# Memory norm and bias table in the second output part of the first feed-forward, memory tiles read once more and split in the third; a later norm row and other weight splits in the second feed-forward

## The chip, the cores and the metric

The kernel runs on one core of a Trainium2 chip. The metric is the device time of one execution in microseconds (us); smaller is better. A core has TensorE (PE) for matrix products, VectorE (DVE), ScalarE (ACT) and GpSimd (POOL) for elementwise work, and SyncE (SP), which here only issues DMAs. The engines run side by side and meet at semaphores.

## The reference

One decoder layer on x (512 tokens, 1024 features) in float32:

```python
x = x + 0.5 * swiglu(rms_norm(x, norm_ffn1_w), ffn1_w_in, ffn1_w_out)      # d_ff 2816
x = x + hybrid_mixer(rms_norm(x, norm_mix_w), ...)                         # SSD heads and attention heads
x = x + memory_cross_attention(rms_norm(x, norm_cross_w), rms_norm(mem, norm_mem_w), w_cq, w_ck, w_cv, w_co)
x = x + 0.5 * swiglu(rms_norm(x, norm_ffn2_w), ffn2_w_in, ffn2_w_out)
return rms_norm(x, norm_final_w)
```

Three details matter. `mem` has 256 rows of 1024 features, and its norm and its key product `rms_norm(mem) @ w_ck` depend on nothing that is computed before them. The attention heads add a bias looked up by relative position from a table of 32 buckets and 8 heads, and subtract a second softmax scaled by `lam`, a scalar made from four small parameter vectors. The root mean square that each norm divides by needs all 1024 features of a token.

## The kernel before, in words

**Layout and arithmetic.** Activations lie transposed, features on partitions: x is 8 tiles of 128x512. Every product is made in three float32r passes from a high and a low part of both operands (`mm3`, L261): high by high, high by low, low by high. So every weight tile (128x1024, 512 KB) is loaded raw by SP into `wr` (6 buffers), its high part `wh` is made by ACT (L149, 3 buffers) and its low part `wl` by DVE from `wr` and `wh` (L150, 3 buffers). An activation is split the same way, `gh` and `gl` for the gated values of a feed-forward, `hnh` and `hnl` for a normed x, `hm` for the memory.

**First feed-forward.** Its 22 tiles of hidden features go in thirds of 8, 8 and 6 (`THIRDS`). A third has quads (L223), products in a Strassen manner: seven products `m1`, `t`, `t+m3`, `m2`, `m7`, `m3`, `t` of summed weights with summed activations. The weight sums are made by accumulating DMAs on POOL's queue (L219) and by DVE (L245, L247), and before the second product ACT copies the first, `qb<-qa` (L241). Behind the last quad comes the gate chain: `gate` on DVE (L385), `th` on ACT (L386), two more steps on DVE (L387, L389), then `gh` on ACT and `gl` on DVE, two tiles of each. Then the output part of that third: for each of 8 output tiles o a product `po` of `nf` weight blocks with the `nf` gated tiles, 24 matmuls of 512 columns in the first two thirds and 18 in the last, and an update of x[o]. The gated tiles of the last quad are only needed by the last quarter or third of each product.

**Statistics.** `Stat` (L318) collects squares: ACT makes `nacc` or `nsq` (L328, L331), DVE adds (L332). `finish` turns the sum into a row: PE sums over partitions into `nps`, DVE makes `nv` (L302), POOL raises it to the power -0.5 (`ncol`, L304), and 2.5 us of planned PE time later `row_of` makes `ch` and `cl` on DVE, two diagonal tiles `ndiag` (one on DVE, one on POOL, L315), two matmuls `nrow`, and ACT copies `nrow` into `row` (L343). `normed` (L348) does this for the mixer's norm and then makes 8 pairs `hf`, `hnh`, `hnl`.

**Beside the third output part** the function `beside` (L457) spawns two chains of small work. `prepare` (L480) loads `lamv`, `rel_sb` and `hot`, makes `lam`, and makes the bias table: one matmul `prel` (L501), an ACT copy `rel_row` (L503), a small DMA to `rel_d` in DRAM and a DMA of 2.5 MB from there to `rel_z` (L506), both on POOL's queue; the attention reads `rel_z` later. `memory_prep(hm, True)` (L862) reads the 8 memory tiles (128x256) by DMAs on POOL's queue, each held in program order behind the accumulating DMAs issued so far (`last_sum`), adds their squares to `st_mem`, splits each into `hm`, and finishes the memory's norm row. Later, in the mixer, `memory_prep(hm2, False)` reads the tiles again.

**After it** comes `memory_keys` (L875): 8 products `pck` of 24 matmuls with 256 columns. It needs `hm` from the start and `st_mem.row` only at `ckf` (L882), after the products. While PE does these keys, the mixer's norm is made by `normed`, spawned at the last x update with a delay of 3.0. Then the mixer begins with the products `pq` of `hn`.

**Second feed-forward.** The norm's row is finished by `st_2.finish()`, spawned 3.0 after the last update (L1008), while the first quad runs; the row is needed at the first gate. Its last third is laid out by token so that the final norm is at hand: `Close.load` splits the left halves of the first two raw weights into `wfh` and `wfl`, `Close.finish` (L1036) splits the other left halves in its loop over f, and then all six right halves.

**What sets the order.** Dense generators yield after each group of matmuls; `Order` (L53) keeps a planned PE time `od.t`, which each matmul advances, and steps the spawned chains when their due time has come. A tile scheduler then orders the instructions of PE, DVE, ACT and POOL by its own estimate, and each engine executes its list strictly in that order. SP alone keeps the order in which the code issues. `tc.issue_after(i)` makes the scheduler place an instruction behind i in the list.

## Time and profile before

| | |
|---|---|
| median of 3 runs | 1359.58 us (1359.15 to 1363.79) |
| profiled execution | 1359.36 us, of which the profile's span is 1357.6 us |
| mean granted TensorE clock | 0.993 |
| PE busy in the span | 1325.9 us, 98% |
| DVE, ACT, POOL busy | 952.6, 631.9, 106.5 us |
| DMA traffic | 166.84 MB, mean 123 GB/s |

The table of busy times says which engine could bound the kernel; which one does, and where it is held up, is told by the table of PE's waits (what each wait ended on, and how long), by windows cut at the stages (busy time of each engine in a stretch of the span, with the clock granted to TensorE) and by the timeline (start and duration of each instruction, and in brackets the idle time before it and what ended it). In these views a line number is that of the kernel, and L140, L149 and L150 are helpers, so the tile names tell the instructions apart. The span leaves out 1.76 us of the execution, before the first and after the last recorded instruction.

### The profile page before, as it was taken

To read this page: it belongs to the slowest core of one execution; us is meant where nothing else is said; L and a number is where in the kernel's file an instruction comes from. 1 tells how busy PE (TensorE), PEld (TensorE's weight loads), DVE (VectorE), ACT (ScalarE), POOL (GpSimd) and SP (SyncE) were. 2 spreads that over 40 slices of the span, in tenths; PEclk is the share of its full clock that TensorE was granted. 3 is DMA by queue.
4 is the path that set the end of the run, shared out by engine and by line. 5 is a ranking of instruction groups with operands and counts; after the bars stand their busy time and mean duration, and the time that the engine had idled before them with its cause. 6 is when DMAs were issued, how large, how long until landed. Compare 5 with 4: busy or idle time off the path is not lost.

```text
span 1357.6 us, 19860 instructions
## 1 busy us (share of the span) xinstructions
PE 1325.9 (98%) x7829; PEld 1150.3 (85%) x7829; DVE 952.6 (70%) x1480; ACT 631.9 (47%) x1069; POOL 106.5 (8%) x130
## 2 busy tenths in 40 slices
PE   8999999998989999999999999999999999999997
PEld 7888999897777778877788887889889989998995
DVE  6874787577767577647867877656788757875765
ACT  6442454244444464536644656434445424542544
POOL 1000000011020001000011031000001000000000
PEclk9999999999989999999999999999999999999999
DMA  7435574463542213432163665321347645745631
GB/s 265 111 120 127 125 201 133 117 187 103 203 154 70 84 51 61 141 109 62 40 124 102 94 123 157 109 78 63 83 104 181 179 129 128 195 137 124 174 106 62
DMA packets 50157, 166.84 MB, mean 123 GB/s; under 512 B 6464, under 2 KB 6872, under 8 KB 50064
## 3 DMA queue, kind: packets, MB, share of 16 engines
q1 hardware_dynamic: 40704, 134.57, 31.2%
q0 software_dynamic: 9360, 31.01, 13.6%
q8 instruction: 61, 1.00, 0.3%
q14 instruction: 32, 0.26, 0.1%
HBM read 163.41 MB, written 4.77 MB: 124 GB/s over the span
## 4 chain that ended last, share of the span: by engine, by line
PE 88%; DVE 3%; DMA 2%; ACT 2%; issue 1%; POOL 1%; POOLq 0%; ACTq 0%; DVEq 0%
PE po L140 17%; PE qb L211 12%; PE pm L140 8%; PE qe L211 7%; PE qa L211 7%; PE pxbc L140 7%; PE pq L140 3%; PE pk L140 3%; PE pcq L140 3%; PE pv L140 3%; PE pz L140 3%; PE pf L140 2%; PE pck L140 2%; PE pg L140 2%; PE pu L140 2%; PE ps L140 2%
## 5 line engine op out<-in xcount | busy, mean ns | idle before, releaser
L149 ACT ACTIVATE wh<-wr 128x1024 fp32r<-128x1024 f32 (+2 forms) x285 | 292.2, 1028 | 391.0 <-PE po L140 129.5
L150 DVE TENSOR_TENSOR wl<-wr,wh 128x1024 fp32r<-128x1024 f32 (+2 forms) x285 | 339.2, 1191 | 105.0 <-ACT wh L149 102.8
L140 PE MATMUL po<-gh,wh 128*128 128x512 f32 x304 | 119.4, 395 | 4.3 <-ACT gh L149 2.4
L140 PE MATMUL po<-gl,wh 128*128 128x512 f32 x304 | 119.0, 394 | 0.0
L140 PE MATMUL po<-gh,wl 128*128 128x512 f32 x304 | 118.8, 393 | 0.0
L211 PE MATMUL qa<-hmh,wl 128*128 128x256 f32 x304 | 86.3, 284 | 0.0
L211 PE MATMUL qa<-hml,wh 128*128 128x256 f32 x304 | 86.0, 283 | 0.0
L211 PE MATMUL qa<-hmh,wh 128*128 128x256 f32 x304 | 86.0, 283 | 0.0
L441 DVE TENSOR_TENSOR upd<-po,row 128x512 f32<-128x512 f32 x40 | 27.7, 691 | 78.8 <-PE po L140 78.8
L140 PEld LDWEIGHTS po<-gh,wh 128*128 128x128 f32 x304 | 57.3, 190 | 18.0 <-ACT gh L149 4.6
L140 PEld LDWEIGHTS po<-gl,wh 128*128 128x128 f32 x304 | 57.6, 190 | 13.1 <-DVE gl L150 1.2
L140 PEld LDWEIGHTS po<-gh,wl 128*128 128x128 f32 x304 | 57.6, 189 | 12.0 <-DVE wl L150 0.3
L211 PEld LDWEIGHTS qa<-hmh,wl 128*128 128x128 f32 x304 | 58.3, 192 | 0.4 <-DVE wl L150 0.4
L211 PEld LDWEIGHTS qa<-hml,wh 128*128 128x128 f32 x304 | 58.3, 192 | 0.2
L211 PEld LDWEIGHTS qa<-hmh,wh 128*128 128x128 f32 x304 | 58.3, 192 | 0.2
L140 PE MATMUL pxbc<-hnh,wh 128*128 128x512 f32 x128 | 52.3, 409 | 0.0
L140 PE MATMUL pxbc<-hnh,wl 128*128 128x512 f32 x128 | 50.3, 393 | 0.0
L140 PE MATMUL pxbc<-hnl,wh 128*128 128x512 f32 x128 | 50.3, 393 | 0.0
L219 POOL DMA_DIRECT2D wr<-in_f2q x22 | 19.1, 870 | 363.3 <-DVE wl L150 110.4
L628 ACT ACTIVATE ec<-ec,mn 128x512 f32<-128x512 f32 (+3 forms) x64 | 35.4, 556 | 25.5 <-DVE mn L627 25.5
L211 PE MATMUL qb<-s12h,wh 128*128 128x256 f32 x152 | 43.3, 285 | 3.5 <-ACT qb L241 3.5
L211 PE MATMUL qe<-s12h,wh 128*128 128x256 f32 x152 | 43.3, 285 | 1.2 <-ACT s12h L149 1.1
(375 smaller groups left out, 3780.4 us busy)
## 6 DMA issues: line engine op xcount, KB each, us to landing
wr<-in_f2q SPq DMA_DIRECT2D x55, 512.0 KB, 4.2
wr<-in_f1q SPq DMA_DIRECT2D x40, 512.0 KB, 4.0
wr<-in_f2q POOLq DMA_DIRECT2D x22, 512.0 KB, 6.3
wr<-in_f2o SPq DMA_DIRECT2D x22, 512.0 KB, 4.2
wr<-in_f1q POOLq DMA_DIRECT2D x16, 512.0 KB, 6.4
wr<-in_f1o SPq DMA_DIRECT2D x16, 512.0 KB, 4.2
wr<-in_wxbc SPq DMA_DIRECT2D x16, 512.0 KB, 3.5
wr<-in_f1i SPq DMA_DIRECT2D x8, 512.0 KB, 6.9
```

The source lines that it names most:

```text
L140: nc.tensor.matmul(out, w, x, start=start, stop=stop)
L149: S.activation(hi, src, AF.Copy),
L150: V.tensor_tensor(lo, src, hi.bitcast(F32), ALU.subtract),
L211: nc.tensor.matmul(out, a_[:, wc], b_, start=first and f == 0 and kp == 0 and j == 0, stop=kp == n - 1 and j == 2, skip_group_check=True)
L219: last_sum[:] = [G.dma_start(raw, m, accum_op=ALU.add).ins]
L441: V.tensor_tensor(upd, po, row4, ALU.mult)
L628: S.activation(ec[:, :n], ec[:, :n], AF.Exp, bias=mn, scale=-1.0, accum_out=sm[c][:, i : i + 1])
```

## The change

Five edits, all in the order of the work; the number of matmuls, of ACT and of DVE instructions stays the same (7674, 951 and 1482 in the program), POOL issues 8 DMAs more.

1. `prepare` and the memory's norm are spawned at the second output part (`ti == 1`) and no more at the third. The memory's preparation is cut in two: `memory_norm` reads the 8 tiles, squares and sums them and makes the row; `memory_prep(hm)` reads the 8 tiles again and splits them, at the third output part as before. With `hm2` the tiles are now read three times in all.
2. The tiles' DMAs stand behind the last accumulating DMA as before (`last_sum`), and their work on ACT and DVE stands behind the last weight split (`recent`).
3. `rel_row` goes; ACT copies `prel` into the first 8 partitions of `hot`.
4. `Stat.finish` takes the distance between `nps` and `nrow` as an argument: 6.0 for the memory, 8.0 for the second feed-forward's norm, which is spawned 5.0 instead of 3.0 after the last update. For the mixer's norm it stays 2.5.
5. In `Close.finish` four of the six right halves are split within the loop over f, the other two after it.

```diff
     def load_w(src, n=D):
...
-            split_into(hi, lo, raw)
+            recent[:] = [i.ins for i in split_into(hi, lo, raw)]
         return hi, lo
+
+    @contextmanager
+    def behind(ins):
+        with ExitStack() as after:
+            for i in ins:
+                after.enter_context(tc.issue_after(i))
+            yield
...
-        def finish(self):
+        def finish(self, apart=2.5):
...
-            yield 2.5
+            yield apart
...
     def beside(ti):
-        if ti == len(THIRDS) - 1:
+        if ti == 1:
             od.spawn(prepare())
-            od.spawn(memory_prep(hm, True))
+            od.spawn(memory_norm())
+        elif ti == 2:
+            od.spawn(memory_prep(hm))
...
-        rel_row = s2("rel_row", shape=(8, T))
-        S.activation(rel_row, prel, AF.Copy, scale=-8.0)
-        nc.gpsimd.dma_start(rel_d[:, :T], rel_row)
+        S.activation(hot[:8], prel, AF.Copy, scale=-8.0)
+        nc.gpsimd.dma_start(rel_d[:, :T], hot[:8])
...
-    def memory_prep(dst, first):
+    def memory_tile(k):
+        mk = s2("mem", shape=(P, MEM))
+        with behind(last_sum):
+            nc.gpsimd.dma_start(mk, a["memT"][k])
+        return mk
+
+    def memory_norm():
         for k in range(KT):
-            mk = s2("mem", shape=(P, MEM))
-            with tc.issue_after(last_sum[0]):
-                nc.gpsimd.dma_start(mk, a["memT"][k])
-            if first:
+            mk = memory_tile(k)
+            with behind(recent):
                 st_mem.add(mk)
-            dst.append(split("hm", mk, par[:, C_MEM + k : C_MEM + k + 1], True))
             yield 2.0
-        if first:
-            yield 3.0
-            yield from st_mem.finish()
+        yield 3.0
+        yield from st_mem.finish(6.0)
+
+    def memory_prep(dst):
+        for k in range(KT):
+            mk = memory_tile(k)
+            with behind(recent):
+                dst.append(split("hm", mk, par[:, C_MEM + k : C_MEM + k + 1], True))
+            yield 2.0
...
-            od.spawn(st_2.finish(), 3.0)
+            od.spawn(st_2.finish(8.0), 5.0)
...
+            w2 = []
             for f in range(nf):
                 if f + 2 < nf:
                     w.append(split("wf", self.raw[f + 2][:, :T]))
+                if f > 1:
+                    w2.append(split("wf", self.raw[f - 2][:, T:]))
...
-            w = [split("wf", self.raw[f][:, T:]) for f in range(nf)]
+            w2 += [split("wf", self.raw[f][:, T:]) for f in range(nf - 2, nf)]
```

What this does to the engines' lists shows at three places. Two `wh` in a row belong to two consecutive weight tiles.

ACT, at the end of the last quad of the second third: the splits of the first three output weights, the gate's `th`, the splits of the last gated tiles. Before:

```order
L149 ACTIVATE wh_2203<-wr_2201 128x1024
L149 ACTIVATE wh_2237<-wr_2235 128x1024
L149 ACTIVATE wh_2271<-wr_2269 128x1024
L386 ACTIVATE th_2185<-gate_2184 128x1024
L149 ACTIVATE gh_2192<-th_2185 128x512
L149 ACTIVATE gh_2196<-th_2185 128x512
```

And after the change, where `nacc` and `nsq` are squares of two memory tiles and `hot<-prel` is the copy of the bias row:

```order
L149 ACTIVATE wh_2203<-wr_2201 128x1024
L335 ACTIVATE nacc_2233<-mem_2231 128x256
L338 ACTIVATE nsq_2249<-mem_2247 128x256
L393 ACTIVATE th_2185<-gate_2184 128x1024
L149 ACTIVATE gh_2192<-th_2185 128x512
L149 ACTIVATE gh_2196<-th_2185 128x512
L511 ACTIVATE hot_2226<-prel_2291 8x512
L149 ACTIVATE wh_2267<-wr_2265 128x1024
```

Two weight splits moved from ahead of `th` to behind `gh`, and the copy of `prel` now stands ahead of the second output's weight. At the third output part the reverse happens: there ACT's list has three splits of 128x768 ahead of `th` after the change.

ACT, at the first quad of the third that follows (the first `wh` is that of `m1`, `qb<-qa` waits for the product `m1`, the `wh` behind it is that of `t`). Before:

```order
L149 ACTIVATE wh_2485<-wr_2472 128x1024
L149 ACTIVATE wh_2516<-wr_2474 128x1024
L149 ACTIVATE wh_2547<-wr_2474 128x1024
L149 ACTIVATE wh_2579<-wr_2479 128x1024
L241 ACTIVATE qb_2514<-qa_2484 128x512
```

After the change:

```order
L149 ACTIVATE wh_2570<-wr_2557 128x1024
L248 ACTIVATE qb_2599<-qa_2569 128x512
L338 ACTIVATE nsq_2325<-mem_2323 128x256
L149 ACTIVATE wh_2601<-wr_2559 128x1024
L338 ACTIVATE nsq_2342<-mem_2340 128x256
L149 ACTIVATE wh_2632<-wr_2559 128x1024
L149 ACTIVATE wh_2664<-wr_2564 128x1024
```

The splits of the second and third weight of the quad moved behind the copy that waits for the first product, with two squares between them.

DVE, at the memory keys, where the mixer's norm row is made (`ch`, `cl`, `ndiag`) and the first `hf` follow. Before:

```order
L882 TENSOR_TENSOR ckf_3893<-pck_3827,row_3501 128x256
L527 TENSOR_TENSOR wdts_3970<-wdt_3968,wdts_3970 128x8x16
L150 TENSOR_TENSOR wl_4023<-wr_4020,wh_4022 128x1024
L309 CAST ch_3635<-ncol_3591 128x4
L311 TENSOR_TENSOR cl_3637<-ncol_3591,ch_3635 128x4
L315 TENSOR_TENSOR ndiag_3640<-ident,ch_3635 128x512
L355 SCALAR_TENSOR_TENSOR hf_3648<-x_79,par,row_3646 128x512
L355 SCALAR_TENSOR_TENSOR hf_3650<-x_83,par,row_3646 128x512
```

After the change:

```order
L150 TENSOR_TENSOR ck_3628<-ckf_3626,ck_3628 128x256
L316 CAST ch_3650<-ncol_3606 128x4
L318 TENSOR_TENSOR cl_3652<-ncol_3606,ch_3650 128x4
L899 TENSOR_TENSOR ckf_3631<-pck_3556,row_2484 128x256
L322 TENSOR_TENSOR ndiag_3655<-ident,ch_3650 128x512
L150 TENSOR_TENSOR ck_3633<-ckf_3631,ck_3633 128x256
L150 TENSOR_TENSOR wl_3774<-wr_3771,wh_3773 128x1024
L362 SCALAR_TENSOR_TENSOR hf_3663<-x_79,par,row_3661 128x512
L362 SCALAR_TENSOR_TENSOR hf_3665<-x_83,par,row_3661 128x512
L899 TENSOR_TENSOR ckf_3759<-pck_3636,row_2484 128x256
L150 TENSOR_TENSOR wl_3804<-wr_3801,wh_3803 128x1024
```

Before, the row's steps stood behind the `wl` of the weight that follows the keys, and so behind all of the keys' work; now they stand among it, on PE after 62 of the keys' 192 matmuls, and the `hf` follow between the `ckf`.

SP's list keeps its length; `lamv`, `rel_sb` and `hot` stand among the second output part's weights in it. On POOL the first 8 memory tiles, `rel_d` and `rel_z` stand ahead of the accumulating DMAs of the last third's first quad.

More of the change, by code (lines that the diff above doesn't have):

```diff
@@ L1 @@
-from contextlib import ExitStack
+from contextlib import ExitStack, contextmanager
 from itertools import chain, islice
@@ L132, in dump @@
             nc.sync.dma_start(dbg[name], t.bitcast(F32) if t.dtype == R32 else t)
-    last, start, last_sum = [], [], []
+    last, start, last_sum, recent = [], [], [], []
     V, S, G = nc.vector, nc.scalar, nc.gpsimd
@@ L697, in out_attn @@
         if prep:
-            od.spawn(memory_prep(hm2, False), 0.0)
+            od.spawn(memory_prep(hm2), 0.0)
         yield lambda: all(y is not None for y in ya[4 * hg : 4 * hg + 4])
@@ L1055, in finish @@
                     for f in range(nf if n else 0):
-                        mm3(po, g[f], w[f], f == 0, f == nf - 1, wc=slice(tb * P, (tb + 1) * P))
+                        mm3(po, g[f], w2[f], f == 0, f == nf - 1, wc=slice(tb * P, (tb + 1) * P))
                         yield
```

## The prediction

> **What bounds the kernel now.** I read the page's busy times first, then the chain that ended last, then the table of PE's waits, then windows cut at the stages that the change touches, and the timeline at each place.
>
> ```profile
> PE 1325.9 (98%) x7829; PEld 1150.3 (85%) x7829; DVE 952.6 (70%) x1480; ACT 631.9 (47%) x1069; POOL 106.5 (8%) x130
> PE 88%; DVE 3%; DMA 2%; ACT 2%; issue 1%; POOL 1%; POOLq 0%; ACTq 0%; DVEq 0%
> ```
>
> PE is busy in 98% of the span and carries 88% of the last chain. Since the change keeps every matmul, it can only act on the remainder: on PE's waits, and on stretches in which PE runs slowly.
>
> ```profile
> PE nrow L140 <- DVE ndiag L315: 4.2, 2, 3.3
> PE qb L211 <- ACT qb L241: 3.5, 3, 2.5
> PE po L140 <- ACT gh L149: 2.4, 1, 2.4
> PE po L140 <- ACT wh L149: 1.8, 1, 1.8
> PE pf L140 <- ACT wfh L149: 1.2, 1, 1.2
> ```
>
> The columns are total, times and longest. Most lie in the third output part, the start of the mixer and the second feed-forward. Windows at the stages, PE only in what I use (busy, matmuls), then the granted clock (0.50 is half speed):
>
> ```profile
> 240.00:260.00 20.00, 20.00 (x90) 16.55 (x89) 8.51 (x10) 3.26 (x4) 0.87 (x1) 1.00 0.58 151
> 284.00:304.00 20.00, 20.00 (x169) 20.00 (x168) 17.06 (x20) 10.76 (x13) 2.08 (x3) 1.00 0.69 181
> 329.09:371.69 42.60, 38.37 (x155) 29.62 (x153) 30.52 (x47) 18.30 (x29) 3.05 (x4) 0.92 0.44 152
> 371.69:395.61 23.92, 23.92 (x201) 23.87 (x199) 15.34 (x21) 9.93 (x12) 2.51 (x2) 1.00 0.58 194
> 395.61:419.28 23.67, 18.15 (x70) 12.34 (x69) 18.82 (x32) 11.65 (x20) 5.78 (x4) 0.86 0.25 72
> 330.85:334.27 3.42, 1.15 (x6) 0.61 (x4) 2.52 (x3) 0.74 (x2) 0.00 (x0) 1.00 0.00 0
> 334.27:337.68 3.41, 3.25 (x7) 1.87 (x8) 2.09 (x4) 1.43 (x4) 0.00 (x0) 0.50 0.00 0
> 310.43:313.84 3.41, 1.60 (x14) 1.40 (x12) 2.02 (x2) 3.41 (x5) 0.54 (x1) 1.00 0.21 67
> ```
>
> The first two give PE's undisturbed rate: 90 matmuls of 512 columns in 20 us (the window's ends cut two), so 0.227 us each, and 169 of 256 columns, 0.12 each. By these the third output part (42.60 us, 8 products of 18 matmuls, 32.7 at the undisturbed rate) loses about 10, and the mixer's first 23.67 us (some 65 matmuls, 14.8) lose about 9. The keys lose nothing. A half-clock stretch costs half of its 3.41 us, 1.7; one follows the stretch in which PE was busy 1.15 us, none follows the one with 1.60 us at 310.43. The mean clocks of 0.92 over 42.60 us and of 0.86 over 23.67 us are about two such stretches each (2 x 0.08 x 42.60 = 6.8 us, 2 x 0.14 x 23.67 = 6.6).
>
> **The change part by part.** I sum against the profiled execution, 1359.36 us; it lies 0.22 under the median, 1359.58, so no correction is made. Plus is slower.
>
> *A, second output part, +4.5 (3 to 6).* In the unchanged kernel the gate chain is covered:
>
> ```profile
> 221.67 0.69 DVE L385 TENSOR_TENSOR gate<-qb,row 128x512 f32<-128x512 f32 x1 [0.68 <-PE qb L211]
> 222.52 1.04 ACT L386 ACTIVATE th<-gate 128x1024 f32<-128x1024 f32 x1
> 226.42 1.15 ACT L149 ACTIVATE gh<-th 128x512 fp32r<-128x512 f32 x2 [2.87 <-DVE th L389]
> 227.11 0.73 PE L140 MATMUL po<-gh,wh 128*128 128x512 f32 x2
> 229.07 1.06 ACT L149 ACTIVATE wh<-wr 128x1024 fp32r<-128x1024 f32 x1 [1.49 <-PE po L140]
> 350.20 0.57 ACT L503 ACTIVATE rel_row<-prel 8x512 f32<-8x512 f32 x1
> ```
>
> From 221.67 to 227.11 PE works on outputs 0 and 1 with the six gated tiles that it has, because three `wh` stood ahead of `th`. Afterwards only that of output 0 does: PE has 18 matmuls, 4.1 us, to about 225.75, and waits until `gh` and `gl` let it go on at about 227.3, allowing 0.2 to 0.3 for the tile's second half: 1.6. Six matmuls and `prel` (0.46) later it needs output 1's weight, but on ACT that stands behind `hot<-prel` (0.57, the `rel_row` row), which waits for `prel`; then `wh` 1.06 and the handovers: a wait of 1.9, and 0.8 more for `wl`, whose 1.23 us are only in part under the first matmuls. That is 1.6 + 0.46 + 1.9 + 0.8 = 4.8, less 0.3 that this place loses already. Queued behind the waiting copy is only ACT's list of weight splits, and their user is PE.
>
> *B, first quad of the last third, +4.7 (2.1 to 6).* `qb<-qa` waits for product `m1`, and the split for `t` now stands behind it:
>
> ```profile
> 269.37 0.58 ACT L241 ACTIVATE qb<-qa 128x512 f32<-128x512 f32 x1
> 271.28 1.06 ACT L149 ACTIVATE wh<-wr 128x1024 fp32r<-128x1024 f32 x1 [1.33 <-issue]
> 272.38 1.23 DVE L150 TENSOR_TENSOR wl<-wr,wh 128x1024 fp32r<-128x1024 f32 x1 [1.66 <-ACT wh L149]
> 312.64 0.40 ACT L331 ACTIVATE nsq<-mem 128x256 f32<-128x256 f32 x1
> ```
>
> So PE, done with `m1`, waits 0.58 + 0.40 + 1.06 = 2.0, with the handover 2.1; then for `wl` 1.23 less two matmuls, 1.0; for `t+m3`, whose `wh` stands behind one more square, 0.6; the memory's `nrow` waits 0.4, and its matmuls and `nps` (0.6) came here from the third part. The low end is the first wait alone, the high one 1.3 more for the second split.
>
> *C, a wait that goes, -2.7.* At the third part ACT used to wait for the first memory tile, which had just been asked for:
>
> ```profile
> 310.42 0.42 ACT L328 ACTIVATE nacc<-mem 128x256 f32<-128x256 f32 x1 [6.45 <-DMA mem<-in_memT]
> 314.52 0.39 PE L211 MATMUL qb<-s12h,wh 128*128 128x256 f32 x1 [2.49 <-ACT qb L241]
> mem<-in_memT POOLq DMA_DIRECT2D x16, 128.0 KB, 3.2
> ```
>
> The weight split and `qb<-qa` behind it came late, and PE with them: 2.49 and 0.2 of slow matmuls. Now no square stands there. At the second part the same wait is free: the tiles are asked for early, and 3.2 us to land is far less than ACT takes to reach them. The 8 additional reads go to the same queue at the place where the first reads were, for splits that come later.
>
> *D, third output part, -9.5 (-7 to -9.6).* What the 42.60 us hold beside the matmuls:
>
> ```profile
> 334.43 0.80 PE L140 MATMUL po<-gh,wh 128*128 128x512 f32 x1 [2.44 <-ACT gh L149]
> 337.59 1.04 PE L140 MATMUL prel<-hot,rel_sb 32*8 32x512 f32 x2
> 340.97 0.70 PE L140 MATMUL po<-gh,wh 128*128 128x512 f32 x1 [1.79 <-ACT wh L149]
> ```
>
> Afterwards three splits of 128x768 precede `th`, so PE has outputs 0 (12 matmuls of four gated tiles) and 1 (11) over the gate's wait, 23 x 0.227 = 5.2 us, as long as the chain in A (221.67 to 227.11, 5.4). `prel`, `nps` and `nrow` have left, and with the two waits both half-clock stretches should go. 32.7 + 0.4 = 33.1 against 42.60. The weaker end keeps one half-clock stretch and 0.8 of waits: the `hm` splits still stand in this part.
>
> *E, start of the mixer, -8.2 (-5 to -8.5).* The norm's row now is made among the keys:
>
> ```profile
> 376.52 1.96 POOL L304 TENSOR_TENSOR ncol<-nv,mhalf 128x4 f32<-128x4 f32 x1 [22.21 <-DVE nv L302]
> 399.03 1.60 PE L140 MATMUL nrow<-ndiag,ones_r 128*128 128x512 f32 x2 [3.26 <-DVE ndiag L315]
> 402.76 0.79 PE L140 MATMUL pq<-hnh,wh 128*128 128x512 f32 x1 [2.14 <-ACT hnh L149]
> 403.35 0.74 DVE L355 SCALAR_TENSOR_TENSOR hf<-x,par,row 128x512 f32<-128x512 f32 x1
> 404.01 0.69 DVE L150 TENSOR_TENSOR hnl<-hf,hnh 128x512 fp32r<-128x512 f32 x1
> ```
>
> `ncol` is ready at 378.5, yet `nrow` runs at 399.03, because `ch` stood behind the keys' `wl` on DVE. PE waits 3.26 for it and 2.14 for the first `hnh`, and runs two stretches at half clock; then DVE feeds it an `hn` pair per 0.74 + 0.69. Of the 23.67 us, 14.8 are matmuls; the 8.9 go, less 0.7 for `nrow`'s two matmuls (0.5) and a short wait (0.2) among the keys. DVE must take 0.68 + 8 x 1.43 = 12.1 us into the keys, where 23.92 - 15.34 = 8.6 are free; the last two pairs run over into the start of `pq`, which needs pair k only 0.68 us after pair k-1. The weaker end is that half of those 3.5 us, and the next weight's `wl`, reach PE.
>
> *F, norm row of the second feed-forward, -1.5.*
>
> ```profile
> 1008.70:1011.12 2.42, 1.10 (x6) 1.00 0.01 3
> 1332.62 0.73 PE L140 MATMUL pf<-wfh,gh 128*128 128x512 f32 x2 [1.21 <-ACT wfh L149]
> ```
>
> The first row is the place of the second `nrow` (PE alone): six matmuls of 0.9 us take 2.42. With 33 more matmuls, 4 us, between `nps` and `nrow` the wait goes; the first gate that needs the row is over 10 us later. *G, close, -1.2:* the right halves were split after the loop and PE waited for the first `wfh`; it is now ready before.
>
> *H, clock, +1.5 (0 to 4.5).* The waits of A (1.6 + 1.9 + 0.8 within 6 us) and B (2.1 + 1.0) can leave a 3.41-us stretch below 1.5 us of PE work; I count one stretch of 1.7, somewhat less than certain.
>
> Sum: 4.5 + 4.7 + 1.5 - 2.7 - 9.5 - 8.2 - 1.5 - 1.2 = -12.4, so 1359.36 - 12.4 = 1347.0. All low ends give 1341, and all high ends 1358.6.
>
> Of the rest: `lamv` comes on SP behind one weight load and DVE waits about a microsecond for it, beside PE's queued matmuls; if these were used up, that is part of A's upper end.
>
> **The rivals.**
>
> *No half clock, 1345.5.* If the new waits don't lower the clock, H is nothing. For it: 1.60 us of work sufficed at 310.43, and A's waits are spread. Against it: a wait of 2.44 sufficed at 334.43. By the Trainium skill, page "TensorE: Matmul & The Clock Gate", section "HAM oscillation — how this bites in real kernels", the rule is "no PE-idle gaps >~3.4µs", and as none of the new waits is that long it would have no stretch here; the trace disagrees in that its 2.44-us gap was followed by one.
>
> *The mixer's start gains half, 1354.1.* If DVE falls behind in the keys, PE still waits there: E is -4.1 instead of -8.2, and two more half-clock stretches fall in, +3.0. For it: 12.1 us into 8.6 free. Against it: `pq` consumes slowly.
>
> *The bias table blocks the last third, about 1376.* The table's DMA now is on POOL's queue ahead of the accumulating DMA of `t`:
>
> ```profile
> rel_z<-rel_d POOLq DMA_DIRECT2D x1, 2560.0 KB, 21.5
> wr<-in_f1q POOLq DMA_DIRECT2D x16, 512.0 KB, 6.4
> ```
>
> Issued at about 232.6 (`prel` done at 229.1, its copy, and some 3 us for the small DMA to `rel_d`, as for `mem`), it lands at 254, and `t` at about 260.5; `t` is needed for its split at about 273.8 (`qb<-qa` at 269.37, plus A). So 13.3 us are to spare, and each microsecond beyond costs one. Were it three times as slow (64.5) under the weight loads beside it, `t` would land at 303.5, 29.7 late: 1347.0 + 29.7 = 1376.7. Against it: the 21.5 were taken under load as well.
>
> *The edits do nothing* is excluded for A to E, since the lists above have moved; F and G could be nothing, and that is 2.7.
>
> **How the numbers follow.** The forecast has 0.47, no half clock 0.29, the half gain 0.19, the bias table 0.05. A measurement of this kernel can tell about 0.5% from no change: 1352.8 and 1366.4. The first two cases are faster, 0.76; the third, with its spread, is within 0.5%, 0.19; the last is slower, 0.05. The range from 1341 (all low ends) to 1355 (the half gain and a microsecond) leaves out the table and the far parts of the unknown terms.
>
> **What would show it.** In the changed profile: waits of `po` on `gh` and on `wh` near 226 and 229 together 3.5 to 4.3; a wait of `qb` or `qe` near 271 on `wh` of about 2; no wait of `qb` near 314; about 33 us for the third output part; `nrow` among the keys, and no wait of 2 us of `pq` on `hnh`; neither `nrow` wait near 1000, nor the `wfh` one. I am wrong if the third part or the mixer's start keep their waits, if half-clock stretches multiply, or if POOL's accumulating DMA holds up the last third.

## The result, and the profile after

The changed kernel takes 1349.12 us (median of 6 runs, 1347.30 to 1352.42), the kernel before 1361.24 in the same comparison (6 runs, 1359.15 to 1363.79): the ratio is 0.9914, with a 95% interval of 0.9895 to 0.9933. The forecast was 1347.0, within 1341 to 1355. The profiled execution took 1348.26 us with a span of 1346.1; that of before 1359.36 with 1357.6, so 11.5 us less in the span.

PE's waits in the changed kernel (total, times, longest):

```profile
...
PE py L140 <- DVE r L822: 2.4, 2, 1.9
PE qe L218 <- ACT wh L149: 1.9, 1, 1.9
PE po L140 <- ACT wh L149: 1.6, 1, 1.6
PE po L140 <- ACT gh L149: 1.1, 1, 1.1
...
PE qe L218 <- DVE wl L150: 0.8, 1, 0.8
PE qb L218 <- DVE wl L150: 0.5, 1, 0.5
PE po L140 <- DVE wl L150: 0.5, 1, 0.5
PE nrow L140 <- DVE ndiag L322: 0.5, 1, 0.5
```

The 3.3 us before `nrow`, the 2.1 before `pq`, the 2.5 before `qb` and the 1.2 before `pf` have gone. New are the waits on `wh` and `wl` before `qe` and `qb`, and those of `po` stand in another part than before. `py` waited before too (2.0); the change does not touch it, nor the wait at the very start that the table leaves out here (2.4 in both kernels).

The same stages as windows (start, end and length in us; busy time and, in brackets, instructions of PE, of its weight loads, of DVE, ACT and POOL; the granted clock; the share and rate of DMA); first the unchanged kernel, from the end of the first output part to the end of the second, then the quads of the last third, then the memory keys with the mixer's start to its first attention output:

```profile
140.61:265.18 124.57, 124.56 (x866) 116.52 (x865) 88.19 (x96) 51.73 (x60) 7.00 (x8) 1.00 0.58 152
...
265.18:329.09 63.91, 61.24 (x507) 60.81 (x505) 48.64 (x62) 31.36 (x43) 8.24 (x13) 1.00 0.58 156
...
371.69:449.49 77.80, 72.03 (x417) 59.43 (x415) 53.61 (x116) 35.17 (x65) 8.86 (x7) 0.96 0.35 111
```

The changed kernel, with the third output part in the third row and the keys alone in the fourth:

```profile
139.99:270.60 130.61, 126.78 (x867) 116.63 (x866) 87.70 (x104) 52.07 (x64) 15.28 (x20) 1.00 0.62 172
...
270.60:336.71 66.11, 62.80 (x513) 61.69 (x511) 50.32 (x59) 32.38 (x42) 9.32 (x13) 1.00 0.57 156
336.71:369.70 32.99, 32.99 (x146) 26.88 (x145) 28.02 (x42) 16.84 (x26) 0.00 (x0) 1.00 0.42 126
369.70:394.84 25.14, 24.64 (x203) 24.35 (x202) 23.27 (x36) 14.08 (x19) 8.64 (x6) 1.00 0.55 179
...
369.70:440.24 70.54, 69.55 (x417) 58.32 (x415) 53.38 (x116) 34.40 (x65) 9.21 (x7) 1.00 0.36 117
```

Against before: 6.0 longer in the second third, 2.2 longer in the last third's quads, 9.6 shorter in the third output part (42.60 to 32.99, where PE now is never idle), 7.3 shorter from the keys to the attention. DVE is busy 23.27 of 25.14 us in the keys, against 15.34 of 23.92: the norm's work now stands there. Further on, the second feed-forward takes 1.7 less at its norm row (85.69 to 84.00 from its first product to its first output) and 2.1 less in its close and behind it (266.49 + 8.72 to 264.99 + 8.17). The first 140 us are 0.6 shorter and the rest of the mixer 0.3, which the change does not touch, and the cross-attention is 1.8 longer, of which below. Together: 6.0 + 2.2 - 9.6 - 7.3 - 1.7 - 2.1 - 0.6 - 0.3 + 1.8 = -11.6, the 11.5 of the spans but for rounding.

The second output part, the quad behind it and the norm's row, in the timeline of the changed kernel:

```profile
227.06 0.51 PE L140 MATMUL po<-gh,wh 128*128 128x512 f32 x1 [1.14 <-ACT gh L149]
229.15 1.02 PE L140 MATMUL prel<-hot,rel_sb 32*8 32x512 f32 x2
230.20 0.59 ACT L511 ACTIVATE hot<-prel 8x512 f32<-8x512 f32 x1 [2.67 <-PE prel L140]
230.70 1.04 ACT L149 ACTIVATE wh<-wr 128x1024 fp32r<-128x1024 f32 x1
231.79 0.50 PE L140 MATMUL po<-gh,wh 128*128 128x512 f32 x1 [1.62 <-ACT wh L149]
233.05 0.50 PE L140 MATMUL po<-gh,wl 128*128 128x512 f32 x1 [0.53 <-DVE wl L150]
273.90 0.58 ACT L248 ACTIVATE qb<-qa 128x512 f32<-128x512 f32 x1 [12.91 <-PE qa L218]
275.80 0.39 PE L218 MATMUL qe<-s12h,wh 128*128 128x256 f32 x1 [1.94 <-ACT wh L149]
376.53 0.17 DVE L316 CAST ch<-ncol 128x4 fp32r<-128x4 f32 x1 [0.60 <-POOL ncol L311]
378.68 0.73 PE L140 MATMUL nrow<-ndiag,ones_r 128*128 128x512 f32 x2 [0.50 <-DVE ndiag L322]
```

The first six rows are step A: PE waits for the late `gh`; then ACT waits 2.67 us for the bias row, copies it, splits output 1's weight, and PE waits for that. The next two are step B: ACT idles 12.91 us in front of `qb<-qa`, with the weight of `t` lying ready behind it. The last two are step E: `ch` follows `ncol` within 0.6 us, and `nrow` runs at 378.68 instead of 399.03.

### The profile page after: what moved, and what is told of

It is laid out like the page before. It is cut to its first block, busy times and chain, and to the rows that moved or that the text cites. A ratio compares the mean times of both kernels' runs of the same rounds, so it can differ in the third digit from the quotient of the medians.

```text
span 1346.1 us, 19858 instructions
## 1 busy us (share of the span) xinstructions
PE 1321.8 (98%) x7829; PEld 1148.1 (85%) x7829; DVE 950.7 (71%) x1480; ACT 631.2 (47%) x1069; POOL 114.0 (8%) x138
## 4 chain that ended last, share of the span: by engine, by line
PE 88%; DVE 4%; DMA 2%; ACT 2%; issue 1%; POOL 1%; POOLq 0%; SPq 0%; ACTq 0%; DVEq 0%
PE po L140 16%; PE qb L218 11%; PE pm L140 8%; PE qe L218 7%; PE qa L218 7%; PE pxbc L140 7%; PE pk L140 3%; PE pq L140 3%; PE pcq L140 3%; PE pv L140 3%; PE pz L140 3%; PE pf L140 2%; PE pg L140 2%; PE pu L140 2%; PE ps L140 2%; DMA r<-cum_d 2%
## 5 line engine op out<-in xcount | busy, mean ns | idle before, releaser
L149 ACT ACTIVATE gh<-th 128x512 fp32r<-128x512 f32 x38 | 23.1, 624 | 45.7 <-DVE th L396 45.7
```

The source lines that it names most:

```text
L149: S.activation(hi, src, AF.Copy),
```

## The experiments

Twelve kernels, seven of them run once. Four stage times carry most of it; here they are for all, from one profiled execution each (us), with the matmuls of the keys that PE does ahead of the mixer's norm row, counted in the trace, and the span:

| kernel | second third | quads of the last | third output part | keys to attention | row after, of 192 | span |
|---|---|---|---|---|---|---|
| before | 124.6 | 63.9 | 42.6 | 77.8 | 192 | 1357.6 |
| changed | 130.6 | 66.1 | 33.0 | 70.5 | 62 | 1346.1 |
| prepare_early | 131.3 | 68.9 | 34.4 | 70.3 | 62 | 1353.3 |
| prepare_late | 125.3 | 61.3 | 42.9 | 78.2 | 192 | 1352.8 |
| table_dma_on_act | 124.5 | 66.6 | 45.2 | 76.5 | 78 | 1359.2 |
| row_later | 133.4 | 65.9 | 33.0 | 75.1 | 75 | 1350.1 |
| prepare_later | 126.2 | 66.5 | 33.0 | 70.3 | 62 | 1341.1 |
| heal_both | 126.4 | 67.8 | 33.0 | 70.3 | 62 | 1343.7 |
| table_after_sums | 126.5 | 60.7 | 37.5 | 78.2 | 83 | 1347.0 |
| table_among_tiles | 126.5 | 60.7 | 39.3 | 77.6 | 95 | 1350.9 |
| two_numbers | 129.8 | 62.4 | 33.0 | 70.6 | 62 | 1338.4 |
| copy_on_dve | 131.3 | 66.1 | 33.0 | 70.7 | 62 | 1345.5 |
| squares_not_held | 137.6 | 64.4 | 33.0 | 70.7 | 62 | 1350.2 |
| ffn2_as_before | 133.3 | 65.8 | 33.0 | 70.5 | 62 | 1349.4 |

How far one execution's stage can be trusted shows in the second third: up to its end ffn2_as_before and row_later have the changed kernel's lists on PE, ACT, DVE and POOL and its waits on `gh`, `wh` and `wl`, yet take 133.3 and 133.4 us instead of 130.6. In them PE waits 1.3 and 1.4 us on `lamv`'s chain instead of 0.2 (`lamv` landed 5.4 us after its issue instead of 4.3), and one stretch of 3.41 us at half clock follows the waits of A.

**Which of the two moved chains does what.** My theory at this point, from the lists: the preparation's move brings the mixer's start and both losses. The rival: the memory norm's move frees the mixer's start. One kernel moves the preparation alone, the other all but the preparation.

```diff
 # prepare_early, against the kernel before
-        if ti == len(THIRDS) - 1:
+        if ti == 1:
             od.spawn(prepare())
+        if ti == len(THIRDS) - 1:
             od.spawn(memory_prep(hm, True))
```

> The kernel before, with only the lambda and bias-table preparation spawned at the second output part; the memory norm stays at the third. Theory: the mixer's start depends on where the bias table's DMA stands in POOL's list, so this alone puts the norm row among the keys: the mixer's start loses about 1.5 us instead of 8.9. It also brings the cost in the second output part by itself (about 49 us instead of 43.7) and 2 to 3 us in the first quad behind it (no squares there). Total about 1354 to 1356. Rival: it is the memory norm's leaving the third output part that frees DVE and the mixer's start; then the start still loses about 8.9, only the costs remain, and the total is about 1362 to 1365.

```diff
 # prepare_late, against the changed kernel
         if ti == 1:
-            od.spawn(prepare())
             od.spawn(memory_norm())
         elif ti == 2:
+            od.spawn(prepare())
             od.spawn(memory_prep(hm))
```

> The changed kernel, with only the lambda and bias-table preparation put back to the third output part. Theory: the second output part is back at 43.5 to 44.5 us and the quads behind it lose nothing (61 to 62 us, the third part's wait for a memory tile gone too), but the mixer's start loses about 8.9 us again and the third output part keeps the bias row's matmul and copy (36 to 40 us instead of 32.8). Total 1351 to 1355. Rival: the memory norm's move alone frees the mixer's start: total 1344 to 1347.

They took 1355.09 and 1354.55 us, both as the theory said. The stages of prepare_early (second output part, quads, third output part), and from its keys to the attention:

```profile
223.75:272.66 48.91, 45.40 (x195) 35.71 (x194) 23.36 (x28) 10.96 (x12) 4.33 (x5) 1.00 0.55 166
272.66:341.53 68.87, 63.07 (x507) 62.21 (x505) 50.60 (x58) 33.13 (x45) 6.87 (x11) 0.98 0.53 145
341.53:375.92 34.39, 34.26 (x152) 27.55 (x151) 28.67 (x46) 17.21 (x27) 1.38 (x2) 1.00 0.40 127
...
375.92:446.19 70.27, 69.55 (x417) 58.33 (x415) 53.27 (x116) 34.40 (x65) 8.13 (x7) 1.00 0.36 114
```

And of prepare_late, its third output part, and from its keys to the attention:

```profile
326.75:369.60 42.85, 38.55 (x149) 28.88 (x148) 29.27 (x43) 18.04 (x28) 1.63 (x2) 0.88 0.47 159
...
369.60:447.77 78.17, 72.19 (x417) 59.87 (x416) 53.60 (x116) 35.19 (x65) 8.56 (x7) 0.96 0.33 105
```

The rival falls. The preparation's move alone shortens the third output part (42.6 to 34.4) and the way from the keys to the attention (77.8 to 70.3), and alone costs 6.8 us in the second third. The memory norm's move alone costs 0.7 there, takes away the wait for a memory tile (quads 61.3) and gains nothing further on. The squares are no large part of A or B: prepare_early has both losses without a square there, prepare_late all the squares and neither.

**What sets the mixer's start.** In POOL's list of before, the bias table's DMA stands ahead of the POOL step of the norm, and I took this for what pushes the row behind the keys.

```diff
 # table_dma_on_act, against the kernel before
-        nc.gpsimd.dma_start(rel_z[:, :, :RW], rel_d[:, None, :].to_broadcast([8, P, RW]))
+        nc.scalar.dma_start(rel_z[:, :, :RW], rel_d[:, None, :].to_broadcast([8, P, RW]))
```

> The kernel before, with one edit: the bias table's DMA is issued by ACT instead of POOL. Theory: this DMA's place in POOL's list is what pushed the mixer's norm row behind the keys, so this alone moves it among them: from the first key product to the mixer's first attention output about 70.5 us instead of 77.8, the third output part unchanged or up to 2 us longer, total 1352 to 1355. Rival: the row stood late because the third output part's squares and splits filled DVE: then 77 to 78 us here, total 1359 to 1362.

It took 1360.95 us. The quads of the last third are 2.7 us longer and the third output part 2.6, and both hold more half clock than in the unchanged kernel (3.41 and 13.65 us, against none and 6.83); how much of this ACT's issuing the DMA brings is not shown. The row did move, to 78 of 192 matmuls, so the DMA's place in the list does set it. It does so through the order that the scheduler lays down, and not by holding POOL up: in the unchanged kernel POOL waited 22.21 us for `nv` ahead of `ncol`, with the DMA issued at 353.2, long before. Why the scheduler orders it so is argued from the lists. But of 7 us only 1.3 came, and here PE waits for a key's `wl`:

```profile
PE pck L140 <- DVE wl L150: 2.9, 1, 2.9
```

So both sides were half right: the DMA moves the row, and a row among the keys is not yet the gain. The next kernel asks this alone, in the changed kernel:

```diff
 # row_later, in normed()
-        yield from st.finish()
+        yield from st.finish(5.0)
```

> The changed kernel with the mixer's norm row made 5.0 instead of 2.5 us of planned time behind its sums, so that it stands 9 key matmul rows of 128 later in PE's list. Theory: DVE has just enough room in the keys, so a later row leaves work over: from the first key product to the mixer's first attention output 73 to 78 us instead of 70.5, with a wait on wl; total 1350 to 1355. Rival: it is enough that the row stands among the keys at all: 70.5 to 71.5, total 1347 to 1349.

It took 1351.98 us, and from the keys to the attention:

```profile
373.32:448.39 75.07, 71.12 (x416) 59.55 (x415) 53.56 (x116) 34.62 (x65) 8.62 (x7) 0.98 0.35 110
```

```profile
PE pck L140 <- DVE wl L150: 3.1, 1, 3.1
```

A row 13 matmuls later (75 instead of 62, 1.6 us of PE time at 0.12 each) costs 4.5 us (75.07 against 70.54). The column of the table agrees: 62 gives 70.3 to 70.7 in eight kernels, 75 gives 75.1, 78 gives 76.5, 83 and more 77.6 to 78.2 (with 83 and 95 the memory tiles come late as well). DVE is at 23.27 of 25.14 us with the row at 62; what it can't do within the keys comes out as a wait on `wl` and, behind it, half clock. In row_later two `wl` follow each other on DVE so:

```profile
384.06 1.23 DVE L150 TENSOR_TENSOR wl<-wr,wh 128x1024 fp32r<-128x1024 f32 x1
...
395.71 1.22 DVE L150 TENSOR_TENSOR wl<-wr,wh 128x1024 fp32r<-128x1024 f32 x1
```

Between them DVE makes mostly `hf` and `hnl`, without a pause, and PE waits for the second `wl` until 396.99; in the changed kernel the `wl` stand among the `hf` and `hnl`, at most 2.9 us apart from 378.88 to 390.31. So a full DVE and the order of its list act together here, and the runs do not separate them. This is my second rival's mechanism, and the changed kernel stands just on the good side of it.

**The losses A and B.** First the preparation later, so that its loads come behind the first outputs' weights; then also the table's DMA behind the sums:

```diff
 # prepare_later, against the changed kernel
-            od.spawn(prepare())
+            od.spawn(prepare(), 12.0)
```

> The changed kernel, with the preparation spawned 12 us of planned time later in the second output part; the bias table's DMA stays ahead of the last third's sums. Theory: the second output part loses nothing beside the bias row's matmul (to the last product of that part about 266.5 to 267.5 us from the start instead of 270.6), the first quad behind it still waits for its second weight (2 us and 0.8), total 1343 to 1345. Rival: the 8 squares are what costs: 1347 to 1349.

```diff
 # heal_both: as prepare_later, and in prepare()
-        nc.gpsimd.dma_start(rel_z[:, :, :RW], rel_d[:, None, :].to_broadcast([8, P, RW]))
+        yield 60.0
+        with behind(last_sum):
+            nc.gpsimd.dma_start(rel_z[:, :, :RW], rel_d[:, None, :].to_broadcast([8, P, RW]))
```

> The changed kernel, with the preparation spawned 12 us of planned time later in the second output part, and the bias table's DMA held behind the accumulating DMAs of the last third. Theory: the 5.2 us that the second output part lost and the 4.6 us that the first quad behind it lost were only caused by three small loads and that DMA standing ahead of weights in the planner's order: second output part 44 to 44.5 us, quads of the last third 61.3 to 62, total 1338 to 1341, about 0.984 of the time before. Rival: the 8 squares on ACT cost this time wherever they stand in that part: the total stays at 1346 to 1349.

prepare_later took 1342.99 us (one run), heal_both 1345.75 (5 runs, ratio to before 0.9877, 0.9853 to 0.9901). A is settled: in both, the second third takes 126.2 to 126.4 us, 4.2 to 4.4 less than in the changed kernel, with the 8 squares still in that part; the waits on `gh` and `wh` are gone. The 1.7 to 1.9 that remain against before hold the bias row's matmuls (1.0) and the memory's `nps` (0.5), which came here from the last third. B stays in prepare_later (quads 66.5), so it is not the small loads but the table's DMA that brings it; it was healed in heal_both's list, and its wait was gone. But heal_both missed its forecast of 1338 to 1341, since a wait came in the third quad:

```profile
313.55 1.04 ACT L149 ACTIVATE wh<-wr 128x1024 fp32r<-128x1024 f32 x1
314.64 0.58 PE L218 MATMUL qe<-s12h,wh 128*128 128x256 f32 x1 [3.83 <-ACT wh L149]
```

There the table's DMA stood ahead of that quad's sum. In the changed kernel one sum stands behind it too. The landing times, as the DMA view gives them for windows that hold one issue of `t` or `m7` each: in the changed kernel behind the table and a quad later,

```profile
wr<-in_f1q POOLq DMA_DIRECT2D x1, 512.0 KB, 13.4
...
wr<-in_f1q POOLq DMA_DIRECT2D x1, 512.0 KB, 5.5
```

and in heal_both behind the table:

```profile
wr<-in_f1q POOLq DMA_DIRECT2D x1, 512.0 KB, 18.3
```

So a sum behind the 2.5 MB does land late, as my third rival has it. In the changed kernel it was asked for at 246.5 and landed at 259.9, well before its split at 274.7, as forecast: the 1.94 us of B are ACT's order (the split behind `qb<-qa`), and not the landing. In heal_both it was asked for at 293.3 and landed at 311.6, 0.8 us after PE began to wait (310.8), and ACT, which was not idle before it, split it only at 313.55, behind `th`, `qb<-qa` and `gh` in its list. Split on landing, it would have been ready at about 312.7, so by this estimate half of the 3.83 us is the landing and half the order. Hence the next two, with the table's DMA behind the last sum, and among the memory tiles:

```diff
 # table_after_sums and table_among_tiles: as heal_both, with
-        yield 60.0
+        yield 70.0      # table_after_sums
+        yield 90.0      # table_among_tiles
```

> As heal_both, with the bias table's DMA held behind the last accumulating DMA of the last third, ahead of the memory tiles' second read. Theory: heal_both's 3.8 us wait and its half clock in the third quad were the real price of the 2.5 MB ahead of a sum, and go: quads of the last third 61 to 61.5 us instead of 67.8, the mixer's start as in the changed kernel, total 1336 to 1338.5, 0.982 to 0.984 of the time before. Rival: the memory tiles, now behind the 2.5 MB, come too late for their splits in the third output part: that part 36 us or more instead of 33, total 1340 or more.

> As table_after_sums, with the bias table's DMA after the first two or three memory tiles of the second read. Theory: quads of the last third the same 61 to 61.5 us; the mixer's norm row stands later in the keys (behind 64 key matmuls more than in the changed kernel), so the mixer's start loses 1 to 4 us of what it had gained: total 1338 to 1341. Rival: the norm row's place in the keys has slack, the same as table_after_sums within 1 us.

They took 1349.13 us (6 runs, ratio 0.9918, 0.9897 to 0.9938) and 1352.16 (7 runs, 0.9935, 0.9911 to 0.9959). The quads came out as the theory said, 60.7, the shortest of all; the rest as the rival said, and worse: behind the table the tiles take longer to land, their splits stand later in the lists of ACT and DVE, and the norm's row falls to 83 and 95 of 192. Tiles in table_after_sums, then in the changed kernel:

```profile
mem<-in_memT POOLq DMA_DIRECT2D x7, 128.0 KB, 22.4
```

```profile
mem<-in_memT POOLq DMA_DIRECT2D x8, 128.0 KB, 6.4
```

No wait in the trace of table_after_sums ends on a tile: ACT began the splits at 344.3, some 17 us after the first tiles had landed (issued from 304.6 on), and 17 us into the third output part, against 6 in the changed kernel. So here too the DMA acts through the order of the lists. PE's waits are then on DVE:

```profile
PE pq L140 <- DVE wl L150: 4.3, 1, 4.3
PE po L140 <- DVE upd L448: 2.8, 1, 2.8
```

The table's DMA must be issued early, where only a sum that is needed much later stands behind it. Two numbers of the changed kernel do that, and leave its lists in order at A and B:

```diff
 # two_numbers, against the changed kernel
-            od.spawn(prepare())
+            od.spawn(prepare(), 8.0)
...
 # in memory_norm()
-            yield 2.0
+            yield 1.0
```

> The changed kernel with two numbers changed: the preparation spawned 8 us of planned time later, and the memory norm's tiles 1.0 instead of 2.0 apart. In the lists, two weight splits precede the gate's step again, the bias row and the memory's row are copied where the next weight has long been split, and the bias table's DMA stands behind the first sum of the last third, ahead of the second. Theory: both losses at the second output part and the quad behind it go without the 3.8 us that heal_both paid, since the sum behind the table now is needed some 30 us after the table is issued: second output part 44 to 46 us, quads 60.7 to 61.5, third part and mixer as in the changed kernel, total 1335 to 1338.5, 0.980 to 0.983 of the time before. Rival: the second sum lands after it is needed, quads 64 or more, total 1341 or more.

1343.04 us (6 runs, 1340.15 to 1348.47), ratio to before 0.9881, 0.9850 to 0.9912; the changed kernel's interval, 0.9895 to 0.9933, overlaps its upper part, and the profiled spans are 1338.4 and 1346.1. So it is clearly faster than the kernel before; that it is faster than the changed one rests on one trace of each. It missed the expectation by 4.5 us in the median, in part because one wait came back in the second third, for a reason that neither theory had:

```profile
231.26 0.54 POOL L507 DMA_DIRECT2D rel_d<-rel_far  x1 [13.46 <-DVE rel_far L506]
...
232.94 0.69 DVE L448 TENSOR_TENSOR upd<-po,row 128x512 f32<-128x512 f32 x1 [1.97 <-PE po L140]
...
234.12 0.42 ACT L338 ACTIVATE nsq<-mem 128x256 f32<-128x256 f32 x1 [4.87 <-DMA mem<-in_memT]
...
234.48 1.22 DVE L150 TENSOR_TENSOR wl<-wr,wh 128x1024 fp32r<-128x1024 f32 x1
...
235.76 0.50 PE L140 MATMUL po<-gh,wl 128*128 128x512 f32 x1 [2.40 <-DVE wl L150]
```

PE waits for output 2's `wl`, which stands on DVE behind output 1's update; the update waits 1.97 us for PE's product, and the `wl` follows it without a pause. Its `wh` had been made at 228.21, so the two longer waits in these rows are not what held PE: POOL waited 13.46 us for a small constant that DVE made late, the memory tile's read stood behind that, and ACT's square waited 4.87 us for the tile, ahead of the weights of later outputs. It is the fastest of the profiled ones, and prepare_later (one run) cannot be told from it.

**What else stands in A.** The copy of the bias row taken from ACT; and the squares not held behind the weight splits:

```diff
 # copy_on_dve, against the changed kernel
-        S.activation(hot[:8], prel, AF.Copy, scale=-8.0)
+        V.tensor_scalar(hot[:8], prel, -8.0, None, ALU.mult)
```

> The changed kernel with the copy of the bias row made by DVE instead of ACT. Theory: the second output part's loss has two causes, the two weight splits that stand behind the gate's step (a wait of about 1.1 on gh and 0.2 on gl, which stays) and the copy ahead of output 1's split (1.6 and 0.5 with the time around them, which goes): that part 46.5 to 47.2 us instead of 48.95. Rival: the split itself comes late whatever stands ahead of it: 48.5 to 49.

```diff
 # squares_not_held, in memory_norm() and memory_prep()
-            with behind(recent):
```

> The changed kernel without the hold of the memory's ACT and DVE work behind the last weight split. The squares then stand in the last quads of the second third. Theory: the splits of output weights and the copy of the bias row stand as in the changed kernel, so the second output part still takes 48 to 49.5 us; the quads of the last third lose the two squares between the splits, 65 to 65.6 us instead of 66.1; the first squares may wait for their tile at about 205 us and cost up to 2 us there: total 1346.5 to 1349. Rival: without squares in ACT's list at the second output part the loss there is gone: 44 to 45 us, total 1343 to 1345.

copy_on_dve took 1347.43 us and its second output part 49.80, with a half-clock stretch in it. The wait on `wh` went, so the copy on ACT was its cause; but one as long on `wl` came, 1.6 us. Output 1's `wl` stands on DVE behind output 0's update (from 230.67 to 232.08) and the copy (0.67), though its `wh` was done at 229.88; so the copy is the smaller share of the new wait. The theory's cause holds for the wait on `wh`, its number fails. squares_not_held took 1352.13 us: the squares stood ahead of their tiles' arrival, ACT waited 7.23 us for one, and the second third became 137.6 us with two stretches at half clock in it. So the hold (edit 2) is worth about 4 us by the spans (1350.2 against 1346.1), more than I gave it, though part of that is where the half clock fell. The loss at the second output part stayed (51.35 us), against the rival.

**The second feed-forward.** The norm row's distance and the close put back:

```diff
 # ffn2_as_before, against the changed kernel
-            od.spawn(st_2.finish(8.0), 5.0)
+            od.spawn(st_2.finish(), 3.0)
...
-                if f > 1:
-                    w2.append(split("wf", self.raw[f - 2][:, T:]))
```

> The changed kernel, with the norm row's distances and the close of the second feed-forward as before. Theory: the two waits come back, 1.7 us at the row and 1.5 us in the close, so 3.2 us slower than the changed kernel: about 1351 to 1352, and 0.9935 of the time before. Rival: these waits were of no weight for the end: same as the changed kernel, 0.9914.

1353.26 us (9 runs, 1351.35 to 1360.06), ratio to before 0.9950, 0.9931 to 0.9970. Its waits are the two that the change removes:

```profile
PE nrow L140 <- DVE ndiag L322: 1.5, 2, 1.0
...
PE pf L140 <- ACT wfh L149: 1.2, 1, 1.2
```

In the traces the stages are 1.7, 1.5 and 0.6 us longer than in the changed kernel: 3.8, a third of the gain. The ratios differ by 0.0036, 4.9 us, with intervals that overlap; the forecast was 0.9935 to the 0.9950 measured.

## Why the prediction was right, step by step

The total and the sign held: -12.4 forecast, -11.5 in the spans, and a gain of 0.86% measured by the ratio against 0.91% forecast. That the total came so near is in part luck, as the steps show:

- **A**, +4.5 (3 to 6): +6.0 in the second third, of which 5.2 lie in the output part (48.95 against 43.71) and 0.8 in the quads ahead of it, where the wait on `lamv`'s chain stands. The mechanism is the one forecast, but the waits were smaller, 1.1 on `gh`, 1.6 on `wh` and 0.5 on `wl` where 1.6, 1.9 and 0.8 stood; those on `gh` and `wh` are together 2.7, below the 3.5 to 4.3 named as the sign. By the windows PE is idle 3.8 us (130.61 - 126.78) where it was never idle, and busy 2.2 longer; of these `prel`'s rows are 1.0, where 0.46 was forecast. The last 1.2 I can't assign to rows. The wait on `lamv`'s chain, left in A's upper end, is 0.2 us here and 0.9 to 1.7 in four other kernels; with it and a half-clock stretch the same lists cost 8.7 and 8.8 in ffn2_as_before and row_later, beyond A's upper end.
- **B and C**, +4.7 - 2.7 = +2.0: +2.2. The waits are 1.9, 0.8 and 0.5 where 2.1, 1.0 and 0.6 stood. In the trace three of the first 8 memory tiles stand behind a sum of that quad in POOL's list, not all 8 ahead of it as I read the lists.
- **D**, -9.5: -9.6. PE is not idle in the third output part.
- **E**, -8.2 (-5 to -8.5): -7.3. The mechanism was right, and DVE's room was tighter than the forecast took it: a row 13 matmuls later loses nearly two thirds of the gain (4.5 of 7.3). The forecast's half-gain rival was therefore nearer than its price suggested.
- **F**, -1.5: -1.7. **G**, -1.2: -2.1, of which 0.6 lies behind the last product, which the forecast did not see.
- **H**, +1.5 for one half-clock stretch after the waits of A and B: the profiled execution has none there, but one after the wait of `py` at 812, which the unchanged kernel has without it. So the term came out right by luck: the size was right and the place wrong. Of the other profiled kernels with A's waits, four (ffn2_as_before, row_later, copy_on_dve, squares_not_held) have a stretch in the second output part, and prepare_early has none there.

What A took more than its term (1.5), and E gave less (0.9), is for the larger part set off by G (0.9) and by parts that the change doesn't touch (0.6 and 0.3). Of the sums in the prediction one is off: all high ends give 1358.5, not 1358.6.

The forecast said nothing on what makes E: it read from the lists that the row had moved, and the experiments add that it is the preparation's move, by the place of the table's DMA in POOL's list, and not the memory norm's. That place sets the order; in no run does a wait of PE end on the table's own DMA. Why the planner put two splits behind the gate's step in A is argued from the lists (three small loads stand ahead of those weights in SP's); only that it goes when the preparation comes later was shown.

## What to carry to other kernels

Read a moved step by every list that it enters: here the place of a 2.5 MB DMA in POOL's list decided where a norm row stood 145 us later (233.5 to 378.7), though POOL was not held up by it, and the small loads and the copy of the same chain cost 4.4 of A's 6.0 us where they came to stand. When a wait follows such a move, look whether the transfer was late on the chip or only stood late in a list: in B and in table_after_sums the data had long landed. A step that is moved into a stage where PE never waits paid here only as far as the engine that does it had room there; the busy time of that engine in that window (15.3 of 23.9, then 23.3 of 25.1) says how near the edge it is. An engine that waits in order for something not yet made holds up all that lies ready behind it (ACT 12.91 us in front of `qb<-qa` in B), so put such an instruction behind the work that is due earlier.

## What the runs showed of the hardware

**Half clock.** The stretches of 3.41 us at half clock lie on a grid that is placed differently in each execution, and whether one follows depends on how a wait falls on it. In the changed kernel, a stretch in the second output part with no consequence, and the one at `py` with its half-clock successor:

```profile
230.74:234.15 3.41, 1.83 (x7) 1.22 (x8) 2.38 (x3) 3.41 (x6) 1.68 (x3) 1.00 0.20 50
...
811.00:814.41 3.41, 1.52 (x8) 0.94 (x7) 1.85 (x3) 3.38 (x11) 0.00 (x0) 1.00 0.78 316
814.41:817.83 3.42, 3.42 (x10) 2.10 (x11) 2.77 (x5) 3.42 (x6) 0.00 (x0) 0.50 0.18 69
```

In row_later, the same waits of the second output part as in the first row, on another place of the grid:

```profile
232.77:236.18 3.41, 1.66 (x6) 1.09 (x7) 2.31 (x4) 3.41 (x6) 1.50 (x3) 1.00 0.16 43
236.18:239.59 3.41, 3.41 (x10) 2.61 (x9) 1.96 (x3) 0.32 (x1) 1.24 (x2) 0.50 0.82 225
```

With 1.83 us of PE work in the stretch the clock stayed, with 1.66 and 1.52 it was halved, after waits of at most 1.9 us each. The 1.60 at 310.43 in the unchanged kernel, after which it stayed, says that the bound isn't exact in these numbers. Laid over all fourteen profiles (without their first 15 and last 8 us), the grid shows the same: each of the 22 stretches with under 1.5 us of PE work was followed by half clock, of the 13 with 1.5 to 1.8 us 7 were, and of those above that, where the clock was full, one (copy_on_dve, 2.04 us from 230.20 on). The Trainium skill's rule, page "TensorE: Matmul & The Clock Gate", section "HAM oscillation — how this bites in real kernels", is "no PE-idle gaps >~3.4µs"; in these traces it is too lax, since half clock followed waits of 1.6 and 1.9 us.

Half clock goes with the spread of equal runs: the unchanged kernel's runs beside the experiments took 1355.87 to 1360.30 us at a mean clock of 0.995 and 1364.62 to 1368.59 at 0.988. The changed kernel's six runs do not line up so (1347.30 us at 0.995, 1352.42 at 0.998), and there is one trace of each kernel only; that the grid's place makes these differences is likely, but not shown.

**The queue of POOL's DMAs.** An accumulating DMA of 512 KB behind one of 2.5 MB landed 13.4 us (changed kernel) and 18.3 us (heal_both) after its issue instead of 5.5, and memory tiles of 128 KB 22.4 (table_after_sums) instead of 6.4.
